# A sparse attention stage rearranged: indexer first, selection in parts, row-tile scores

## The chip, the cores and the metric

One program on one core of a Trainium2 chip. The metric is device time in microseconds for one launch, the median of three runs. The core's engines work side by side, each in the order of its own instruction stream: TensorE (PE, matmuls), VectorE (DVE), ScalarE (ACT), GpSimd (POOL), and SyncE (SP), which issues DMA transfers.

## The reference

The program is a chain of seven stages on 512 tokens of 1024 channels, all in float32: a feed-forward block, a hybrid mixer (dilated attention and mLSTM), a second feed-forward block, then a sparse attention mixer, a feed-forward block, a short convolution mixer and a last feed-forward block. The change touches the sparse attention alone:

```
q, k, v, qi, ki, wi = split(h @ w_in)       # 16 q heads, 4 k and v heads of 64;
                                            # 8 indexer heads qi of 64, one ki of 64, 8 weights wi
q = rope(rmsnorm(q));  k = rope(rmsnorm(k))
qi = rope(qi);  ki = rope(layernorm(ki))
for each block j of 128 queries:            # j = 0..3
    score = sum_h wi[:, h] * relu(qi[:, h] @ ki.T)       # (128, 512)
    score = where(causal, score, -inf)
    sel   = top_k(score, 128)               # the 128 best keys of each query
    p     = softmax over the selected, causal keys of q @ k.T / 8   # 4 q heads share a k head
    o     = p @ v
y = o @ w_out
```

Block j needs only its 128(j+1) causal keys, and block 0 needs no selection, since its causal keys are at most 128.

## The kernel before, in words

Activations lie with channels on the partitions and the 512 tokens along the row. A float32 projection is done as three matmuls of split operands (L461 to L463): a weight tile is cast to a high part on ACT (L124) and the rest is subtracted on DVE or POOL (L126). `W.pool_lo` says which: False all on DVE, True every second one on POOL, 2 all on POOL. Raw weights come in 1 MB loads on SP's queue (L101) into a ring of three buffers, so a load waits until the splits of an older one are done.

`proj_T` makes n output chunks of 128 channels; behind each chunk's 24 matmuls it evacuates the PSUM tile and calls `step()`. `step()` runs the callbacks that were put on `deferred` before, and advances the generator at the head of `side_work` by one. So each projection chunk carries a portion of other work, written out in the order in which the engines get it. There is no scheduler; the order in the program is the order on each engine.

The stage, `dsa_block` (L1453 to L1797), goes like this.

- ki and the four qi chunks are projected. `rope` swaps the 32-row halves by DMAs on SP (L1464, L1465), multiplies by cosine and sine on POOL (L1466, L1469), and adds on DVE (L1472). A head has 64 channels, so two heads lie on the 128 partitions of a chunk. For the two heads of a chunk to be scored by 128-partition matmuls, ki is copied on ACT into two tiles padded with zeros (L1526, L1527); the zeros are set on POOL (L1484, L1485). The keys k get the same treatment, eight copies into KZ (L1650, L1651).
- Beside the k and q projections the generator `select` (L1578) issues, in one step, two pairs of indexer products (L1557) and their readers: relu on ACT (L1565), the weighted sum on DVE (L1567, L1569). The top-k selection follows: 16 rounds for each of j = 1, 2, 3. A round is the eight largest of each row (MAX8, L1589) and their replacement by a mark (MATCH_REPLACE8, L1591), over 128(j+1) columns. PLAN sets how many rounds of j = 1 and 2 stand in a step, alternating instruction by instruction where both have some. The rounds of j = 3 come one to a step.
- The order of the projections is k, q (eight chunks), v. q's squares are summed by a matmul into one PSUM tile (L1628), and behind the last q chunk the roots of all are taken at once (L1704 to L1712).
- Attention follows in 32 units (j, hp), hp a pair of heads: first (1, hp) and (2, hp) alternating, then (3, hp) and (0, hp). A unit has scores (L1730), mask, scale and row minimum in one DVE instruction (L1738), exp with its sum on ACT (L364), division on POOL (L1748), transposes (L1757), copies (L1760), the products with v (L1770), and the split of the output (L1774, L1775). The loop is a pipeline: in one turn unit u gets its scores, u−1 its division, u−3 its transposes, u−5 its values. A unit that needs a selection not yet done makes the loop `step()` until it is. The output projection follows (L544).

Of the kernel before, what the change touches and what calls it, by code (L numbers as in the profile page):

```python
# [237 lines left out]
def body(ctx: ExitStack, tc: tile.TileContext, A: dict, consts: bass.AP, out: bass.AP,  # L238
# [11 lines left out]
    cl = ctx.enter_context(tc.tile_pool(name="col", bufs=8))  # L250
# [63 lines left out]
    mhalf = cp.tile([P, 4], F32, tag="mhalf", name="mhalf")  # L314
# [1138 lines left out]
    def dsa_block(layer):  # L1453
# [27 lines left out]
        kiA, kiB = big("U4"), big("U5")  # L1481
        KZ = [(big(f"U{6 + 2 * g}"), big(f"U{7 + 2 * g}")) for g in range(4)]
        def zeros(a, b):
            nc.gpsimd.memset(a[64:128], 0.0)  # L1484
            nc.gpsimd.memset(b[0:64], 0.0)  # L1485

        def evac_qi(c, ps):
            raw = tmp()
            nc.scalar.copy(raw, ps)
            rope(QI[c], raw)  # L1490
            zeros(*KZ[c])

# [3 lines left out]
        def evac_ki(c, ps):  # L1496
            raw = big("F4")
            nc.scalar.copy(raw[0:72], ps[0:72])
            zeros(kiA, kiB)
            x = raw[0:64]  # L1500

            def rest():
# [11 lines left out]
                def more():  # L1514
# [15 lines left out]
                    rope(x, z, 64, last)  # L1530
# [13 lines left out]
        marks = {}  # L1544

        def score(*heads):


            parts = []
            for j, h in heads:  # L1550
                n = P * (j + 1)
                if h == 0:
                    marks[j] = big(f"F{j}")
                both = pb("A") if not parts else None
                for i in range(2):
                    ps = both[:, S * i:S * i + n] if both is not None else pm()[:, 0:n]
                    nc.tensor.matmul(ps, QI[h // 2][:, P * j:P * (j + 1)], (kiA, kiB)[i][:, 0:n],  # L1557
                                     start=True, stop=True)
                    parts.append((j, h + i, ps))
            for j, h, ps in parts:  # L1560
# [18 lines left out]
        def select():  # L1579

            def some_scores():
                if ready and to_score:
                    score(*[to_score.pop(0) for _ in range(min(2, len(to_score)))])

            def rounds(j, n):
                sc = marks[j][:, 0:P * (j + 1)]
                for _ in range(n):
                    m8 = colt((P, 8))
                    nc.vector.max(m8, sc)  # L1589
                    yield  # L1590
                    nc.vector.match_replace(sc, m8, sc, TAKEN)  # L1591
                    yield

            def some_rounds(*many):
                todo = [rounds(*x) for x in many if x[1]]
                while todo:
                    todo = [x for x in todo if next(x, True) is None]

            def taken(j):
                sel[j] = sel_t[:, j - 1] if j < 3 else sel_u[:, 0]  # L1600
                n = P * (j + 1)
                nc.vector.tensor_scalar(sel[j][:, 0:n], marks[j][:, 0:n], -2e38, NEG, op0=ALU.is_gt, op1=ALU.mult)

            while len(to_score) > 8:
                some_scores()
                yield
            for n1, n2 in PLAN:
                some_rounds((1, n1), (2, n2))
                yield
                some_scores()  # L1610
            taken(1)
            taken(2)
            for _ in range(16):
                some_rounds((3, 1))
                yield
            taken(3)
# [5 lines left out]

        def squares(t, ps, start, stop):
            sq = side("acc", (P, S))
            nc.scalar.activation(sq, ps, AF.Square)

            def add():
                nc.tensor.matmul(ss[0:20, 0:S] if t >= 2 else ss[0:20, S:2 * S], zsel[:, t, :], sq,  # L1628
                                 start=start, stop=stop)

            deferred.append(add)

        kraw = [big("F5"), big("F0")]

        def evac_k(c, ps):
            nc.scalar.activation(kraw[c], ps, AF.Copy, scale=cB[:, 73:74])
            squares(c, ps, c == 0, c == 1)
            if c == 0:
                return

            def rest():
                v, y = tmp()[0:4], sp1.tile([P, 768], F32, tag="wide", name=nm("wide"))[0:4, 0:S]
                nc.vector.tensor_scalar(v, ss[0:4, S:2 * S], 1.0 / 64, EPS, op0=ALU.mult, op1=ALU.add)
# [4 lines left out]
                def copies(g):  # L1648
                    (a, b), o = KZ[g], kraw[g // 2][64 * (g % 2):64 * (g % 2) + 64]
                    nc.scalar.copy(a[0:64], o)  # L1650
                    nc.scalar.copy(b[64:128], o)  # L1651
                    if g < 3:
                        deferred.append(lambda: copies(g + 1))

                def more():
                    for t in range(2):
                        p1 = pm()

                        nc.tensor.matmul(p1, kexp[t], y, start=True, stop=True)
                        o, z = kraw[t], side("ada_w", (P, 768))[:, 0:S]  # L1660
                        nc.vector.tensor_tensor(z, o, p1, op=ALU.mult)
                        rope(o, z, then=(lambda: copies(0)) if t else None)

                deferred.append(more)

            deferred.append(lambda: deferred.append(lambda: deferred.append(rest)))

        side_work.append(select())
        W.pool_lo = True
        proj_T("dsa", 2, H, evac_k)  # L1670
        Q = [big(f"U{14 + i}") for i in range(8)]

        def evac_q(c, ps):
            raw = side("ada_w", (P, 768))[:, 0:S]
            nc.scalar.activation(raw, ps, AF.Copy, scale=cB[:, 72:73])
            squares(2 + c, ps, c == 0, c == 7)
            rope(Q[c], raw)

        V = [big("F6"), big("F7")]

        def evac_v(c, ps):
# [3 lines left out]
            def rest():  # L1685
# [3 lines left out]
                for jj in range(2):  # L1689
                    nc.scalar.copy(V[jj].rearrange("p (j c) -> p j c", j=2)[:, :, P * c:P * (c + 1)],  # L1690
                                   pt[:, 256 * jj:256 * (jj + 1)].rearrange("p (j c) -> p j c", j=2))
# [3 lines left out]
        rows, rq = big("F4"), big("R", F32, (P, 80))  # L1695

        def sums_out():
            step()
            nc.scalar.copy(rows[0:20], ss[0:20, 0:S])

        def roots():


            ps = pm()  # L1704
            for j in range(NT):
                nc.tensor.transpose(ps[:, 20 * j:20 * (j + 1)], rows[0:20, P * j:P * (j + 1)], ident[0:20, 0:20])
            v, t = tmp(), tmp()
# [5 lines left out]

        proj_T("dsa", 8, H, evac_q)
        midway.extend([sums_out, roots])
        W.pool_lo = 2
        proj_T("dsa", 2, H, evac_v)


# [213 lines left out]
```

## Time and profile before

| what | value |
|---|---|
| median of 3 runs | 2681.61 us (2677.54 to 2684.05) |
| profiled execution, its own time | 2684.03 us |
| its span, first to last instruction | 2682.3 us, 32412 instructions |
| mean granted TensorE clock | 0.993 of full |
| PE busy over the span | 2635.3 us (98%), 12880 matmuls |
| DVE busy | 1385.7 us (52%) |
| ACT busy | 918.2 us (34%) |
| POOL busy | 541.9 us (20%) |
| DMA | 288.43 MB, mean 108 GB/s |

The sparse attention stage lies between about 1486 and 1740 us of the span; in the page's row of 40 slices its place is the 23rd to 26th slice. Busy shares over the whole span say little about it: the other stages are long runs of projections. Matmul ends in the trace are modelled and overlap, so intervals between starts are used for PE. Lines such as L1730 are lines of the kernel before.

### The profile page before, as it was taken

The numbers are of one execution on the slowest core, as the hardware profiler recorded it, in microseconds if no ns is written. First come the engines' busy times: TensorE is split into PE (matmuls) and PEld (weight loads), VectorE is DVE, ScalarE is ACT, GpSimd is POOL, SyncE is SP. The second block draws the span as 40 slices with busy tenths as digits, with TensorE's granted clock in tenths as the row PEclk, the third lists the DMA queues.
The fourth block names the chain that finished last, engine by engine and source line by source line (L and its number), as shares of the span: only waits on it lengthen the run. The fifth ranks groups of instructions, "written<-read, shape, count | busy, mean of one in ns | idle before, by whom it ended". The sixth has DMA issues, their size and how long they took to land.

```text
span 2682.3 us, 32412 instructions
## 1 busy us (share of the span) xinstructions
PE 2635.3 (98%) x12880; PEld 2174.9 (81%) x12880; DVE 1385.7 (52%) x2072; ACT 918.2 (34%) x1482; POOL 541.9 (20%) x548
## 2 busy tenths in 40 slices
PE   8999999999999999999999899999999999999999
PEld 7888889888777788888888766788888888888887
DVE  5545566375627454665555689453333544533332
ACT  4322233322344433423223436532222332322222
POOL 3211234154112211422123445220000200200000
PEclk9999999999999999999999899999999999999999
DMA  6555443223221323246545131032232322232322
GB/s 187 158 180 185 143 146 118 63 71 95 73 69 48 110 83 122 86 154 199 187 152 160 43 101 60 8 104 87 87 110 75 115 94 96 86 98 83 111 85 71
DMA packets 256474, 288.43 MB, mean 108 GB/s; under 512 B 9924, under 2 KB 238836, under 8 KB 256324
## 3 DMA queue, kind: packets, MB, share of 16 engines
q1 hardware_dynamic: 244196, 234.91, 28.0%
q0 software_dynamic: 10496, 50.95, 6.1%
q8 instruction: 101, 1.65, 0.3%
q10 hardware_dynamic: 1632, 0.52, 0.1%
q14 instruction: 49, 0.40, 0.0%
HBM read 278.59 MB, written 4.19 MB: 105 GB/s over the span
## 4 chain that ended last, share of the span: by engine, by line
PE 90%; DVE 7%; ACT 1%; issue 1%; POOL 1%; DMA 0%; SPq 0%; DVEq 0%; ACTq 0%; POOLq 0%
PE mm L461 25%; PE mm L462 25%; PE mm L463 25%; PE mm L544 2%; PE mm L657 1%; PE mm L659 1%; PE mm L658 1%; PE mm L1730 1%; PE B L1136 1%; DVE X L810 1%; DVE L L696 1%; PE mm L1770 1%; PE A L1279 1%; PE B L1302 1%; DVE F L1591 1%
## 5 line engine op out<-in xcount | busy, mean ns | idle before, releaser
L461 PE MATMUL mm<-H,whi 128*128 128x512 f32 (+1 forms) x2360 | 902.3, 382 | 0.0
L462 PE MATMUL mm<-L,whi 128*128 128x512 f32 (+1 forms) x2360 | 893.7, 379 | 1.4 <-DVE L L696 1.4
L463 PE MATMUL mm<-H,wlo 128*128 128x512 f32 (+1 forms) x2360 | 893.4, 379 | 0.9 <-DVE wlo L126 0.9
L126 DVE TENSOR_TENSOR wlo<-raw,whi 128x1024 fp32r<-128x1024 f32 (+3 forms) x431 | 505.9, 1174 | 555.0 <-ACT whi L124 550.8
L124 ACT CAST whi<-raw 128x1024 fp32r<-128x1024 f32 (+3 forms) x460 | 444.6, 968 | 411.4 <-PE mm L462 332.0
L461 PEld LDWEIGHTS mm<-H,whi 128*128 128x128 f32 x2360 | 445.5, 189 | 91.5 <-issue 10.6
L463 PEld LDWEIGHTS mm<-H,wlo 128*128 128x128 f32 x2360 | 445.3, 189 | 84.2 <-DVE wlo L126 1.6
L462 PEld LDWEIGHTS mm<-L,whi 128*128 128x128 f32 x2360 | 445.8, 189 | 83.6 <-DVE L L696 2.2
L461 PE MATMUL mm<-U,whi 128*128 128x512 f32 (+1 forms) x804 | 312.4, 389 | 0.0
L463 PE MATMUL mm<-U,wlo 128*128 128x512 f32 (+1 forms) x804 | 310.8, 387 | 0.0
L462 PE MATMUL mm<-U,whi 128*128 128x512 f32 (+1 forms) x804 | 310.7, 386 | 0.0
L413 POOL TENSOR_TENSOR acc<-acc,sq 128x512 f32<-128x512 f32 (+1 forms) x74 | 91.9, 1241 | 642.4 <-ACT sq L400 641.7
L670 ACT CAST U<-t 128x512 fp32r<-128x512 f32 x104 | 64.6, 621 | 406.9 <-POOL t L759 194.2
L461 PEld LDWEIGHTS mm<-U,whi 128*128 128x128 f32 x804 | 151.0, 188 | 33.5 <-issue 3.3
L463 PEld LDWEIGHTS mm<-U,wlo 128*128 128x128 f32 x804 | 151.0, 188 | 30.8
L462 PEld LDWEIGHTS mm<-U,whi 128*128 128x128 f32 x804 | 151.0, 188 | 30.2
L671 DVE TENSOR_TENSOR U<-t,U 128x512 fp32r<-128x512 f32 x104 | 72.1, 693 | 134.2 <-ACT U L670 134.2
L882 POOL DMA_DIRECT2D ada_w<-in_ada_w_dram x128 | 71.5, 558 | 281.6 <-DVE wide L906 220.5
L906 DVE SCALAR_TENSOR_TENSOR wide<-ada_w,csilu,wide 128x768 f32<-128x768 f32 x112 | 115.3, 1029 | 16.2 <-DMA ada_w<-in_ada_w_dram 16.2
L126 POOL TENSOR_TENSOR wlo<-raw,whi 128x1024 fp32r<-128x1024 f32 (+1 forms) x29 | 69.5, 2398 | 247.2 <-ACT whi L124 245.6
L757 DVE TENSOR_TENSOR t<-t,mm 128x512 f32<-128x512 f32 x88 | 60.3, 685 | 110.9 <-PE mm L463 110.8
L759 POOL TENSOR_TENSOR t<-t,R 128x512 f32<-128x512 f32 x44 | 56.4, 1283 | 218.4 <-DVE t L757 211.2
(386 smaller groups left out, 2791.7 us busy)
## 6 DMA issues: line engine op xcount, KB each, us to landing
ada_w<-in_ada_w_dram POOLq DMA_DIRECT2D x128, 384.0 KB, 3.6
raw<-in_ffn_w_up_dram SPq DMA_DIRECT2D x44, 1024.0 KB
raw<-in_ffn_w_gate_dram SPq DMA_DIRECT2D x43, 1024.0 KB
raw<-in_w_in_dram SPq DMA_DIRECT2D x30, 1024.0 KB
raw<-in_ffn_w_down_dram SPq DMA_DIRECT2D x32, 768.0 KB
raw<-in_ffn_w_down_dram SPq DMA_DIRECT2D x32, 640.0 KB
raw<-in_w_in_dram SPq DMA_DIRECT2D x24, 512.0 KB
raw<-in_conv_w_in_dram SPq DMA_DIRECT2D x12, 1024.0 KB
```

The costliest lines, as they stand in the source:

```text
L124: nc.scalar.copy(hi, raw)
L126: e.tensor_tensor(lo, raw, hi.bitcast(F32), op=ALU.subtract)
L413: (eng or nc.vector).tensor_tensor(self.acc[:, c], self.acc[:, c], sq[:, c], op=ALU.add)
L461: nc.tensor.matmul(ps, whi, hhi, start=start, stop=False)
L462: nc.tensor.matmul(ps, whi, hlo, start=False, stop=False)
L463: nc.tensor.matmul(ps, wlo, hhi, start=False, stop=stop)
L670: nc.scalar.copy(hi, src)
L671: nc.vector.tensor_tensor(lo, src, hi.bitcast(F32), op=ALU.subtract)
L757: nc.vector.tensor_tensor(s, s, ps, op=ALU.mult)
L759: nc.gpsimd.tensor_tensor(s, s, R, op=ALU.mult)
L882: nc.gpsimd.dma_start(loaded[i], A["ada_w_2"][layer, k * P:(k + 1) * P, 768 * cg:768 * (cg + 1)])
L906: nc.vector.scalar_tensor_tensor(acc, w, csilu[:, k:k + 1], acc, op0=ALU.mult, op1=ALU.add)
```

## The change

Only `dsa_block` changes, the order of its weights, and the number of small buffers. In its order:

- **ki and products.** ki stands once on partitions 0 to 63 and is brought to 64 to 127 by a DMA on SP's queue, in the step in which ki's rotation ends. Products are 64-row tiles: the two heads of a chunk on the two halves of the partitions, each into its own PSUM half, 256 columns at a time. A step issues products (`some_products`), and the next step their readers (`weighed`). The flag `ready` is set one step earlier than before.
- **Selection.** One generator goes through j = 1, 2, 3 in order; each round yields a cost estimate, and `select(much)` runs rounds until a budget is spent: 5.0 a step, 2.4 + 1.6 where units are under way beside q, 1.4 a turn of the loop behind q. j's rounds begin when all its products have been weighed.
- **Keys.** The rotated keys are used as they are; `KS` holds them with the two halves exchanged, by four DMAs on SP.
- **Order.** k, then v, then q. q's squares are matmuls with the squares stationary, into eight columns of PSUM tile B for each chunk; the roots are taken per chunk, by one DVE instruction and five small POOL ones.
- **Units.** Blocks 0 and 1 are one unit, so there are 24: eight (0,1), eight (2), eight (3). Up to six of the first kind start beside the q projections (`beside_q`); their outputs go to `kept` and are split later (`parted`). Scores, too, are row tiles.
- **lo splits.** `W.pool_lo = 2` is gone, so every second split stays on DVE up to the end of the attention.

```diff
@@ plan_dsa
     plan.append(chunk_T("dsa", w, 0, ND, C["k"], 256))
+    plan.append(chunk_T("dsa", w, 0, ND, C["v"], 256))
     plan += [chunk_T("dsa", w, 0, ND, C["q"] + 256 * c, 256) for c in range(4)]
-    plan.append(chunk_T("dsa", w, 0, ND, C["v"], 256))
@@ dsa_block
...
                     def last():
-                        nc.scalar.copy(kiA[0:64], x)
-                        nc.scalar.copy(kiB[64:128], x)
-                        deferred.append(lambda: deferred.append(lambda: ready.append(True)))
+                        nc.sync.dma_start(ki[HALF[1]], ki[HALF[0]])
+                        deferred.append(lambda: ready.append(True))
...
+        def products(heads, ps):
+            j, h = heads
+            n = P * (j + 1)
...
+            for o in range(0, n, 256):
                 for i in range(2):
-                    ps = both[:, S * i:S * i + n] if both is not None else pm()[:, 0:n]
-                    nc.tensor.matmul(ps, QI[h // 2][:, P * j:P * (j + 1)], (kiA, kiB)[i][:, 0:n],
+                    c = slice(o, min(o + 256, n))
+                    nc.tensor.matmul(ps[i][:, c], QI[h // 2][HALF[i], P * j:P * (j + 1)], ki[HALF[i], c],
                                      start=True, stop=True)
...
-        PLAN = ((6, 0), (6, 0), (4, 4), (0, 4), (0, 4), (0, 4))
+        def selection():
+            for j in (1, 2, 3):
+                n = P * (j + 1)
+                while j not in whole:
+                    yield 100.0
+                sc = marks[j][:, 0:n]
+                for r in range(16):
                     m8 = colt((P, 8))
                     nc.vector.max(m8, sc)
                     nc.vector.match_replace(sc, m8, sc, TAKEN)
+                    yield 0.3 + n / 470
...
+            def swapped(t):
+                for i in range(2):
+                    nc.sync.dma_start(KS[t][HALF[i]], kraw[t][HALF[1 - i]])
...
+            def add():
+                both = bank()[:, 384:392]
+                for j in range(NT):
+                    nc.tensor.matmul(both[:, 2 * j:2 * j + 2], sq[:, P * j:P * (j + 1)], zsel[:, 2, 4:6], start=True,
+                                     stop=True)
+                def rest():
+                    v, y, z = colt((P, 8)), colt((P, 8)), colt((P, 8))
+                    nc.vector.tensor_scalar(v, both, 1.0 / 64, EPS, op0=ALU.mult, op1=ALU.add)
+                    nc.gpsimd.tensor_tensor(y, v, mhalf, op=ALU.pow)
...
+                    there[0] = c + 1
...
-        units = [(j, hp) for hp in range(8) for j in (1, 2)] + [(j, hp) for hp in range(8) for j in (3, 0)]
+        units = [((0, 1), hp) for hp in range(8)] + [((2,), hp) for hp in range(8)] + [((3,), hp) for hp in range(8)]
...
         def scores(u):
...
-                nc.tensor.matmul(ps[:, 0:n], Q[hp][:, P * j:n], KZ[hp // 2][i][:, 0:n], start=True, stop=True)
+            for j, o in places(js):
+                n = P * (j + 1)
+                for c in range(0, n, 256):
+                    w = min(256, n - c)
+                    for i in range(2):
+                        nc.tensor.matmul(pss[i][:, o + c:o + c + w], Q[hp][HALF[i], P * j:P * (j + 1)],
+                                         k2[i][HALF[i], c:c + w], start=True, stop=True)
...
+        def beside_q():
+            while True:
+                go(6)
+                go(4)
+                go(1)
+                if parts:
+                    weighed()
+                now = at[0] - at[2]
+                select(2.4 if now else 5.0)
+                go(2)
+                if now:
+                    select(1.6)
+                while adds:
+                    adds.pop(0)()
+                go(5)
+                go(3, at[2] - 1)
+                banks.clear()
+                if sel[1] is not None and at[0] < 6 and there[0] > at[0] + 1:
+                    go(0)
+                some_products()
+                yield
...
+        side_work.append(beside_q())
+        W.pool_lo = True
+        proj_T("dsa", 2, H, evac_k)
+        proj_T("dsa", 2, H, evac_v)
+        proj_T("dsa", 8, H, evac_q)
+        side_work.clear()
...
+        while at[6] < len(units):
+            go(5, now - 4)
+            go(6)
+            go(3, now - 2)
+            go(0)
+            go(2, now)
+            now += 1
+            go(4)
+            if at[1] < len(units):
+                while sel[units[at[1]][0][-1]] is None:
+                    if parts:
+                        weighed()
+                    some_products()
+                    select(2.0)
+            go(1)
+            if waiting:
+                hp = waiting.pop(0)
+                parted(hp, slice(0, 256), kept[hp // 2][:, hp % 2])
+            select(1.4)
             step()
```

`go(stage)` moves the next unit through one of the seven stages scores, softmax, divided, transposed, copied, values, put.

## Rows read from the trace of the kernel before

**Rows 1.** the chain of waits over the whole span: shares by engine.

```profile
PE 90%; DVE 7%; ACT 1%; issue 1%; POOL 1%; DMA 0%; SPq 0%; DVEq 0%; ACTq 0%; POOLq 0%
```

**Rows 2.** stretches: start:end, length; busy us of PE, PEld, DVE, ACT, POOL; PEclk.

```profile
1535.00:1558.00 23.00, 18.44 (x69) 12.71 (x68) 11.88 (x16) 11.63 (x21) 9.18 (x9) 0.93 0.42 123
1558.00:1665.00 107.00, 101.54 (x453) 65.08 (x453) 100.62 (x256) 56.11 (x134) 53.15 (x49) 0.97 0.28 82
1665.00:1718.00 53.00, 52.92 (x418) 35.27 (x419) 28.17 (x125) 42.42 (x149) 22.31 (x42) 1.00 0.01 1
```

**Rows 3.** DVE by line and form, 1558 to 1665: busy us, mean ns.

```profile
L1589 DVE MAX8 col<-F 128x8 f32<-128x512 f32 x16 | 11.0, 688 | 0.0
L1591 DVE MATCH_REPLACE8 F<-col,F 128x512 f32<-128x512 f32 x16 | 10.8, 676 | 0.0
...
L126 DVE TENSOR_TENSOR wlo<-raw,whi 128x1024 fp32r<-128x1024 f32 x4 | 7.3, 1818 | 1.3 <-ACT whi L124 1.3
L1738 DVE CUSTOM_DVE_ANT_0 t<-mm,U,R 128x384 f32<-128x384 f32 x12 | 6.9, 606 | 0.1
...
L1738 DVE CUSTOM_DVE_ANT_0 acc<-mm,U,R 128x256 f32<-128x256 f32 x7 | 3.3, 467 | 0.0
```

**Rows 4.** DVE in time (start us, us): first rounds, last round.

```profile
1558.01 0.41 DVE L1589 MAX8 col<-F 128x8 f32<-128x256 f32 x1
...
1558.98 0.43 DVE L1589 MAX8 col<-F 128x8 f32<-128x256 f32 x1
...
1663.96 0.68 DVE L1591 MATCH_REPLACE8 F<-col,F 128x512 f32<-128x512 f32 x1
```

**Rows 5.** PE in time: steady units, then the output projection's first matmul.

```profile
1669.94 1.46 PE L1730 MATMUL mm<-U,U 128*128 128x384 f32 x4
1671.32 0.32 PE L1770 MATMUL mm<-wide,F 128*64 128x128 f32 x1
...
1672.84 1.88 PE L1730 MATMUL mm<-U,U 128*128 128x512 f32 x4
...
1677.79 1.88 PE L1730 MATMUL mm<-U,U 128*128 128x512 f32 x4
...
1717.23 0.92 PE L544 MATMUL mm<-H,whi 128*128 128x256 f32 x3
```

**Rows 6.** PE in time, two 4-row tiles side by side, in the mix stage.

```profile
756.74 0.69 PE L1257 MATMUL A<-rc,cst 4*128 4x512 f32 x1
756.74 0.69 PE L1258 MATMUL A<-rc,cst 4*128 4x512 f32 x1
757.27 0.59 PE L1257 MATMUL A<-rc,cst 4*128 4x512 f32 x1
```

**Rows 7.** all engines in time around ki (SPq: SP issuing a DMA).

```profile
1531.57 3.79 DVE L126 TENSOR_TENSOR wlo<-raw,whi 128x1024 fp32r<-128x1024 f32 x1 [1.66 <-ACT whi L124]
...
1535.28 0.68 DVE L1472 TENSOR_TENSOR F<-F,t 64x512 f32<-64x512 f32 x1
...
1538.47 0.58 SPq L101 DMA_DIRECT2D raw<-in_attn_w_in_dram  x1
...
1539.23 0.51 SPq L1464 DMA_DIRECT2D t<-t  x1
...
1545.52 1.29 POOL L1469 TENSOR_TENSOR t<-t,rs 128x512 f32<-128x512 f32 x1 [1.86 <-DMA t<-t]
```

**Rows 8.** waits of SP's queue, 1535 to 1720: us in total, times, longest.

```profile
SPq L101 <- POOL wlo L126: 13.1, 1, 13.1
```

**Rows 9.** PE in time at 1535, and the stretch behind it (PEclk eighth).

```profile
1534.77 0.39 PE L462 MATMUL mm<-L,whi 128*128 128x512 f32 x1
1534.99 0.39 PE L463 MATMUL mm<-H,wlo 128*128 128x512 f32 x1
1539.92 1.89 PE L1628 MATMUL B<-acc,dsa_consts 128*20 128x512 f32 x2 [4.54 <-ACT acc L1625]
...
1540.00:1550.00 10.00, 9.98 (x34) 6.59 (x35) 5.34 (x8) 3.35 (x8) 4.83 (x5) 0.83 0.75 233
```

More of the change, by code (lines that the diff above doesn't have):

```diff
@@ L1574, in score, with some_products @@
                                             compare_op=ALU.is_ge, fill=NEG)
-        PLAN = ((6, 0), (6, 0), (4, 4), (0, 4), (0, 4), (0, 4))
+                    whole.append(j)
+            parts.clear()
+        whole = []
         to_score = [(j, h) for j in (1, 2, 3) for h in (0, 2, 4, 6)]
[L1579 to L1587, printed above, removed]
+        def some_products():
+            if not ready or not to_score:
+                return
+            if to_score[0][0] == 1:
+                both = pb("A")
+                for k in range(2):
+                    products(to_score.pop(0), [both[:, S * i + 256 * k:S * i + 256 * (k + 1)] for i in range(2)])
+            else:
+                both = pb("A")
+                products(to_score.pop(0), [both[:, S * i:S * (i + 1)] for i in range(2)])
@@ L1611, in select @@
[L1611 to L1616, printed above, removed]
+                yield 0.5
+        selecting = selection()
+        def select(much):
+            while much > 0:
+                cost = next(selecting, None)
+                if cost is None:
+                    break
+                much -= cost
         ss = pb("B")
@@ L1646, in rest @@
                 newton(y, v, 1.0, tmp()[0:4])
[L1648 to L1670, printed above, removed]
+                deferred.append(lambda: more(y))
+            def add():
+                nc.tensor.matmul(ss[0:20, 0:S], zsel[:, c, :], sq, start=c == 0, stop=c == 1)
+                if c:
+                    deferred.append(rest)
+            deferred.append(add)
         Q = [big(f"U{14 + i}") for i in range(8)]
+        there = [0]
+        rq = big("R", F32, (P, NT, 16))
         def evac_q(c, ps):
@@ new lines, in divided, with width, transposed @@
+        def divided(u):
+            prs, l, some = probs[u]
+            nc.vector.reciprocal(l[:, 0:len(some)], l[:, 0:len(some)])
+            for k, pr in enumerate(some):
+                nc.gpsimd.tensor_scalar(pr, pr, l[:, k:k + 1], 0.0, op0=ALU.mult, op1=ALU.add)
+        def width(u):
+            return sum(P * (j + 1) for j in units[u][0])
+        def transposed(u):
+            ps = bank() if phase[0] else pb("AB"[u % 2])
+            for i, pr in enumerate(probs.pop(u)[0]):
+                for b in range(0, width(u), P):
+                    nc.tensor.transpose(ps[:, S * i + b:S * i + b + P], pr[:, b:b + P], ident)
+            turns[u] = ps
@@ L1777, in dsa_block @@
-        for u in range(len(units) + 5):
-            if 0 <= u - 5:
-                values(u - 5)
-            if 0 <= u - 3 < len(units):
-                transposed(u - 3)
-            if 0 <= u - 1 < len(units):
-                divided(u - 1)
-            if u < len(units):
-                while sel[units[u][0]] is None:
-                    step()
-                scores(u)
+            for x, (j, o) in enumerate(places(js)):
+                for b in range(j + 1):
+                    for i in range(2):
+                        nc.tensor.matmul(ob[64 * i:64 * i + 64, P * x:P * (x + 1)],
+                                         V[b // 2][:, 256 * (b % 2) + 64 * kv:256 * (b % 2) + 64 * kv + 64],
+                                         pts[i][:, o + P * b:o + P * (b + 1)], start=(b == 0), stop=(b == j))
@@ new lines, in dsa_block, with go @@
+        kept, waiting = {}, []
+        phase = [True]
+        stages_of_units = (scores, softmax, divided, transposed, copied, values, put)
+        at = [0] * len(stages_of_units)
+        def go(stage, most=len(units)):
+            if at[stage] < min(most, at[stage - 1] if stage else len(units)):
+                stages_of_units[stage](at[stage])
+                at[stage] += 1
+        def beside_q():
[19 more added lines that the diff above has]
+                yield
```

209 lines of the change are left out of this document (102 added, 107 removed).

## The prediction

> **What bounds the kernel now.** I read the chain of waits first: TensorE (PE) carries nine tenths of the chain that ended last, VectorE (DVE) most of the rest [rows 1]. The change lies in one stage, sparse attention, so I then cut that stage into stretches. The reader is to see two regimes [rows 2]. From 1558 to 1665 DVE is busy 100.6 of 107 us: the top-k rounds run from 1558.0 to 1664.6 [rows 4]. PE is busy 101.5 us there, but much of that is matmuls that found their operands just in time, and its clock is below full (0.97). From 1665 on DVE is busy 28 of 53 us and PE 52.9 of 53, up to the output projection at 1717.2 [rows 5]. So the stage is DVE-bound, then PE-bound: saved matmul time counts at full only behind the last round, and anything on DVE counts before it. A third place is a hole of 4.5 us on PE at 1535, after which 1540 to 1550 runs at a mean granted clock of 0.83, between its two levels (1.2 and 2.4 GHz) [rows 9].
>
> **The change, part by part.**
>
> *PE work behind the last round.* In the steady part a (j=2) unit costs 1672.84 − 1669.94 = 2.90 us of PE: 1.38 scores (to 1671.32), 1.52 values and transposes [rows 5]. Less 0.10 that I take for the change of shape, its four 384-column passes (two heads, two passes each in float32) make 1.28, 0.32 a pass; four of 512 columns by that 4 × 0.43 = 1.72. A (3)+(0) pair takes 4.95 us (1672.84 to 1677.79). After, a head's scores contract over 64 partitions instead of 128, two heads side by side on the two halves. What two side-by-side tiles cost stands in the trace once: two 4-row tiles of 512 columns start together, and the next pair starts 757.27 − 756.74 = 0.53 us later [rows 6], where two full passes take 0.86. That is 61%; some of the 0.53 I put down to the change of shape around it and take 56%. So a (2) unit costs 0.72 + 0.10 for the change of shape + 1.52 = 2.34, and a (3) unit, scaled by 4/3, 0.96 + 0.10 + 2.03 = 3.09. The Trainium skill (TensorEngine Tiling (Array Packing), section Overview, Theoretical Speedup) promises up to a factor 2 for a contraction of at most 64; the one pair in this trace shows 1.6. With the factor 2 the sum below ends 1.3 us earlier.
>
> *DVE work up to the last round.* Rounds keep their number, 16 for each of three blocks, 0.97 us at 256 columns [rows 4], 0.69 + 0.68 plus a load of the eight values, about 1.45, at 512 [rows 3]. Before interleaves part of j=1 and j=2, which I read as hiding some issue gaps; the sequential form loses them: +2.3 us, and nothing at the least. The lo splits: POOL takes all of them from the v projection on in before; now they alternate to the end, so DVE gets one more before its last round: 7.3/4 = 1.8 us [rows 3], at most two, 3.6. Softmax: before does 12 (2) and 13 (1) heads' reductions in this stretch (0.61 and 0.47 us each [rows 3]). After must, by my reading of the budgets (two rounds at 1.4 in the tail), have done about eight (0,1) units and one or two (2) units when the last round ends. A (0,1) unit takes 2 × 0.47 + 2 × 0.33 (0.47 less the 0.14 that 128 columns make between the two rows) + four readouts and a reciprocal, about 0.5, = 2.1 us, plus the split of its output: together +3 us. Rope adds, relu accumulation, k's Newton steps and the per-q roots (eight small DVE instructions against five) cost what they did. Sum +7 us on 107. Before's idle share (6.4 us) I take as a third smaller, since steps are larger and readers come a step later: −2.
>
> *When the rounds start.* After, the first products are issued a step earlier, right behind k0's projection, but need ki in its second partition half, brought by a DMA on SP's queue. ki's add ends at 1536.0 (DVE came to it only after a lo split that took 3.79 us beside two POOL instructions) [rows 7]. In order behind it on SP stand qi2's transfers, a 1 MB weight load issued at 1538.5, and qi3's transfers at 1539.2, whose reader on POOL starts at 1545.5 [rows 7]. The swap is issued between that load and qi3's transfers; they ran behind the load's packets, so I put it at about 1542.8. PE, ready at about 1529.7, would wait 13 us instead of 4.5, with k1's projection behind it. It costs little, since DVE starts its rounds at about 1557 in either: products (1,4) and (1,6) come right behind k1's projection, near 1552, as in before, and before's first round waited for a lo split. Bounds: the swap lands at once, rounds 5 us earlier; it lands behind a second load, 5 us later. What is late next is k1, by 8 us, covered by PE's slack in the DVE-bound stretch.
>
> *PE in that stretch.* Indexer products halve (about −7 us), q's squares become eight small matmuls per chunk, about the same; k, v and q still make eleven projections behind k0's first. A projection is 24 matmuls that start 0.22 to 0.23 us apart [rows 9], 5.45 us. Before, PE had from 1535 on ten of them (54.5), 16 unit pairs of (1) and (2) and of (3) and (0) at some 4.9 (79), and 29 for products, squares and small things: 162. After, from 1529.7 on: eleven (60), 16 units of 2.34 and 8 of 3.09 (62), products 9.4, the rest 12.5: 144. Nothing of it shows while DVE is the bound.
>
> *POOL and ACT.* Ten POOL memsets and ten ACT copies vanish, five small POOL instructions per q come. POOL is busy 53 of 107 us [rows 2], so they are hidden, unless they hold DVE up: DVE's lo split took 3.79 us beside POOL against 1.8 on average [rows 3, 7]. The Trainium skill (SBUF — State Buffer, section on the two separate sides) says that DVE and GpSimd share a port pair as an exclusive lock and that the loser blocks for the whole instruction; the trace agrees in that row. By that rule 40 more POOL instructions would stretch DVE's two-input ones; with a quarter of DVE's time in such, an estimate of 4 us later. The sum leaves it out.
>
> *Sum.* Last round: 1557 + 107 + 7 − 2 = 1669. Then 14 units lack scores, 17 transposes, 19 values: 6 × 2.34 + 8 × 3.09 = 38.8, plus 3 × 0.75 + 5 × 0.8 = 6.3 for the older units (half of a (2) unit's 1.52 each), plus 1 for the drain: 46.1. End 1715.1 against 1717.2: −2.1. The profiled execution took 2684.0 (span 2682.3 and 1.7 around it), 2.4 above the median of 2681.6; so 2681.9 by it, and **2680 on the median**.
>
> Both ends: with perfect overlap PE never waits but for ki's swap, and the stage ends at 1529.7 + 144 + 13 = 1687, −30. If 12 us of DVE work more than I see come in front, +10.
>
> **The rivals.**
>
> *R1, faster: selection goes under the projections and PE, not DVE, sets the end.* For it: DVE's 114 us fit beside eleven projections and the units if rounds are spread well; up to six (0,1) units run beside q and bring PE work into what was slack. Against it: j=3's selection can't start until all its products are in, about q7. By 1529.7 + 144 + 13 + some 10 of remaining waits the stage ends at 1697: −20, **2661**.
>
> *R2, slower: the swaps on SP's queue starve DVE.* Besides ki's, four transfers turn k's halves, also on SP, also between weight loads; in before SP once stood 13.1 us at a load that waited for a lo split on POOL [rows 8]. If a swap is issued behind such a load, the first scores stop PE, the projections and products behind them wait, and DVE runs out of work after one step's budget, about 6 us. It decides from a wait of some 9 us at the scores; a 13.1 us wait costs about 7 net, two of them or one plus a later ki about 12: **2692**. Against it: k's swaps are issued four or more projections before their readers.
>
> *R3, row tiles do not run side by side.* Then the 14 units' scores cost 6 × 0.56 + 8 × 0.76 = 9.4 us more: **2689**. For it: the tiles of the trace have 4 rows and stream 512 columns, these have 64 and 256. Against it: two tiles on different partitions did start together [rows 6].
>
> *R4, the change doesn't do what it says:* no unit starts beside q, because sel[1] or the roots come too late. Then DVE has the same work in another order: 2683.
>
> **How the numbers follow.** No change 0.44 (own range 2670 to 2690), R1 0.31, R2 0.12, R3 0.09, R4 0.04. Less than 0.3% (8 us) is not to be told from nothing. Faster: R1 and 0.08 of the first, 0.39. Slower: R2, 0.06 of R3, 0.04 of the first, 0.22. Same: 0.39. The range reaches from a good R1 to R2, 2656 to 2698.
>
> **What would show it.** In the profile after: the first round near 1557 and the last near 1669 (R1: before 1655; R2: after 1675); PE's wait at the first products about 13 us, released by a DMA; a (3) unit at 3.1 us of PE (R3: 3.9); about 14 units' scores behind the last round; other stages unchanged. The forecast is wrong if the rounds' stretch is far from 112 us or if PE waits behind it.

## The result, and the profile after

The changed kernel takes 2709.7 us in the median (2706.7 to 2711.0), against 2682.2 for the kernel before: a ratio of 1.0104, 95% interval 1.0086 to 1.0121. It is 27.5 us slower. The forecast was no change, at 2680, with a range up to 2698.

The two traces first need a common mark. ACT's copy of ki out of PSUM stands at the same place of both programs, in the kernel before and in the kernel after at:

```profile
1512.13 0.58 ACT L1498 COPY F<-mm 72x512 f32<-72x512 f32 x1 [2.52 <-PE mm L463]
```

```profile
1506.34 0.58 ACT L1498 COPY F<-mm 72x512 f32<-72x512 f32 x1 [2.50 <-PE mm L463]
```

So a time of the trace after is read 5.8 us later to compare it with a time of the trace before or of the forecast. The change does not make this shift: over the nineteen traces of this document the copy lies anywhere between 1505.3 and 1512.5, in versions of either kernel.

The stretches of the profile after that answer to [rows 2]; columns as there, PEclk the eighth: first round to last round, then up to the output projection.

```profile
1554.40:1693.10 138.70, 107.77 (x561) 82.49 (x559) 107.28 (x271) 52.73 (x139) 73.68 (x99) 0.82 0.23 67
1693.10:1740.00 46.90, 46.06 (x473) 36.02 (x473) 26.51 (x97) 39.19 (x112) 20.06 (x32) 1.00 0.01 2
```

DVE's work between the rounds is 107.3 us, against 100.2 to 100.6 before: the +7 of the forecast, though not from the terms that it was added up from (see below). The part behind the last round is 46.9 us, forecast 46.1. What is wrong is the length of the first line: 138.7, not 112. DVE stands idle for 31 us of it (before: 6), PE too, and PE's mean granted clock there is 0.82 (before: 0.97).

From ki's copy to the output projection, the kernel before and the kernel after:

```profile
1512.13:1717.20 205.07, 194.99 (x1048) 130.78 (x1046) 153.78 (x405) 118.86 (x314) 96.99 (x112) 0.98 0.22 66
```

```profile
1506.34:1740.00 233.66, 188.67 (x1189) 144.18 (x1187) 158.50 (x394) 109.34 (x279) 111.24 (x143) 0.86 0.21 60
```

PE's busy time fell by 6 us only, and much of it now runs at a lower granted clock (0.86 in the mean, 0.98 before); its idle time grew from 10 to 45 us. The sum is 28.6 us, near the 27.5 of the medians. The two spans (2682.3 and 2704.9) differ by 22.6, which is 28.6 less the shift of 5.8 ahead of the stage.

Where PE waits in the profile after, 1554.4 to 1693.1 (total, times, longest):

```profile
PE B L1681 <- DVE col L1686: 13.0, 2, 10.8
PE B L1785 <- DVE col L1774: 6.8, 1, 6.8
PE B L1681 <- ACT U L1796: 6.0, 2, 4.3
PE mm L1748 <- DVE L L671: 2.9, 1, 2.9
```

and where DVE waits in the same stretch:

```profile
DVE col L1605 <- POOL F L1575: 9.1, 3, 5.4
DVE F L1571 <- ACT sq L1567: 6.0, 4, 1.8
DVE L L671 <- ACT H L670: 4.2, 2, 3.0
```

The longest wait shows how the two stop each other. DVE in time (start, duration, and in brackets the idle time before it):

```profile
1579.34 0.29 DVE L1609 TENSOR_SCALAR U<-F 128x256 bf16<-128x256 f32 x1
...
1588.05 4.05 DVE L1571 SCALAR_TENSOR_TENSOR F<-sq,wcol,F 128x384 f32<-128x384 f32 x2 [1.41 <-ACT sq L1567]
1597.50 0.56 DVE L1605 MAX8 col<-F 128x8 f32<-128x384 f32 x1 [5.40 <-POOL F L1575]
```

```profile
1603.64 1.22 DVE L126 TENSOR_TENSOR wlo<-raw,whi 128x1024 fp32r<-128x1024 f32 x1
1604.77 1.29 DVE L1472 TENSOR_TENSOR F<-F,t 128x512 f32<-128x512 f32 x2
...
1605.97 0.69 DVE L1472 TENSOR_TENSOR U<-U,t 128x512 f32<-128x512 f32 x1
1606.57 0.16 DVE L1686 TENSOR_SCALAR col<-B 128x8 f32<-128x8 f32 x1
...
1606.88 0.77 PE L1681 MATMUL B<-dsa_consts,acc 128*128 128x2 f32 x3 [10.75 <-DVE col L1686]
```

j=1's rounds are done at 1579.3 (L1609 is its `taken`). j=2's can't start before its four pairs of products, issued one pair a step, have been weighed and POOL has set the causal mask (L1575): 1597.5, 18 us later. (Before j=3's rounds there is a second such hole, of 10.9 us.) Then five rounds, a lo split and three rope adds stand ahead of L1686, the read that frees PSUM tile B for PE's next squares. PE has been done with its projection since 1596 and waits till 1606.9. The clock follows:

```profile
1590.00:1600.00 10.00, 6.13 (x30) 4.49 (x26) 4.36 (x8) 4.02 (x6) 8.38 (x11) 1.00 0.43 133
1600.00:1610.00 10.00, 3.12 (x16) 3.05 (x18) 9.62 (x22) 0.00 (x0) 2.86 (x6) 0.54 0.26 62
1610.00:1620.00 10.00, 10.00 (x48) 7.80 (x47) 8.29 (x22) 3.92 (x13) 8.76 (x9) 0.78 0.07 17
1660.00:1670.00 10.00, 4.94 (x24) 3.48 (x24) 5.77 (x25) 4.76 (x19) 9.67 (x13) 0.50 0.37 117
```

Idle PE, a granted clock near its lower level, and work after that at 0.78. The same at 1660 to 1670, where the last q chunks come through POOL (9.67 of 10 us busy).

At the start PE waits 5.3 us for ki's rope add on DVE (L1472) and, as forecast, another 7.9 for ki's exchange (L1525), which stands on SP's queue behind a weight load:

```profile
1529.47 1.22 PE L1555 MATMUL A<-U,U 64*128 64x256 f32 x2 [5.32 <-DVE U L1472]
...
1531.93 0.58 SPq L101 DMA_DIRECT2D raw<-in_attn_w_in_dram  x1
1532.62 0.56 SPq L1525 DMA_DIRECT2D U<-U  x1
...
1538.60 2.07 PE L1555 MATMUL A<-U,U 64*128 64x256 f32 x6 [7.90 <-DMA U<-U]
```

The units themselves came out well. PE in the steady part, answering to [rows 5]: first a (2) unit, then a (3) unit, each from its first score matmul to that of the next.

```profile
1705.05 0.48 PE L1748 MATMUL mm<-U,U 64*128 64x256 f32 x1
1705.06 0.48 PE L1748 MATMUL mm<-F,U 64*128 64x256 f32 x1
1705.37 0.38 PE L1748 MATMUL mm<-U,U 64*128 64x256 f32 x1
1705.38 0.38 PE L1748 MATMUL mm<-F,U 64*128 64x256 f32 x1
...
1705.59 0.27 PE L1748 MATMUL mm<-U,U 64*128 64x128 f32 x1
...
1707.52 0.48 PE L1748 MATMUL mm<-U,U 64*128 64x256 f32 x1
...
1727.34 0.48 PE L1748 MATMUL mm<-U,U 64*128 64x256 f32 x1
...
1730.46 0.48 PE L1748 MATMUL mm<-U,U 64*128 64x256 f32 x1
...
1739.97 0.62 PE L544 MATMUL mm<-H,whi 128*128 128x256 f32 x3
```

A (2) unit takes 2.47 us (forecast 2.34, before 2.90), a (3) unit 3.12 (forecast 3.09). Two heads' passes of 256 columns, started 0.01 us apart, together take 0.22 us (1705.37 to 1705.59), where one head's 384 took 0.32 before, or 0.21 for 256. That is the full factor of 2 that the Trainium skill (TensorEngine Tiling (Array Packing), Overview, Theoretical Speedup) names as the upper end; here the trace agrees with it.

### The profile page after: what moved, and what is told of

The parts are those of the page before. It is cut to its first block, busy times and chain, and to the rows that moved or that the text cites. A ratio compares the mean times of both kernels' runs of the same rounds, so it can differ in the third digit from the quotient of the medians.

```text
span 2704.9 us, 32602 instructions
## 1 busy us (share of the span) xinstructions
PE 2625.6 (97%) x13020; PEld 2186.4 (81%) x13020; DVE 1389.4 (51%) x2060; ACT 908.7 (34%) x1447; POOL 554.0 (20%) x577
## 4 chain that ended last, share of the span: by engine, by line
PE 88%; DVE 7%; POOL 1%; ACT 1%; issue 1%; DMA 1%; SPq 0%; DVEq 0%; ACTq 0%; POOLq 0%
PE mm L461 25%; PE mm L462 25%; PE mm L463 25%; PE mm L544 2%; PE mm L657 1%; PE mm L658 1%; PE mm L659 1%; DVE col L1605 1%; DVE F L1606 1%; PE B L1136 1%; DVE X L810 1%; DVE L L696 1%; PE mm L1748 1%; PE mm L1807 1%; PE A L1279 1%
```

## The experiments

Medians, and ratios to the kernel before that ran on the same chip, with 95% intervals:

| run | us | ratio |
|---|---|---|
| after | 2709.7 | 1.0104 (1.0086 to 1.0121) |
| 2 rounds, after | 2684.2 | 1.0009 (0.9999 to 1.0018) |
| 2 rounds, before | 2673.6 | 0.9968 (0.9959 to 0.9978) |
| 2 rounds, after, exchanges on ACT's queue | 2673.8 | 0.9974 (0.9963 to 0.9985) |
| half budget | 2693.0 | 1.0045 (1.0030 to 1.0060) |
| quarter budget | 2693.7 | 1.0043 (1.0027 to 1.0060) |
| two pairs of j=2 in a step | 2696.4 | 1.0051 (1.0036 to 1.0066) |
| read before rounds | 2700.9 | 1.0072 (1.0057 to 1.0087) |
| exchanges on ACT's queue | 2706.6 | 1.0090 (1.0075 to 1.0105) |
| half budget + exchanges | 2686.8 | 1.0021 (1.0011 to 1.0031) |
| half budget + exchanges + two pairs | 2687.9 | 1.0020 (1.0011 to 1.0030) |
| no units beside q | 2707.8 | 1.0094 (1.0075 to 1.0112) |
| no units beside q, v last | 2708.4 | 1.0104 (1.0088 to 1.0119) |
| the same, read first, budget 4.0 | 2698.7 | 1.0070 (1.0053 to 1.0087) |
| roots off POOL | 2713.6 | 1.0124 (1.0109 to 1.0139) |
| four edits | 2696.7 | 1.0063 (1.0048 to 1.0078) |
| row tiles in the old order | 2680.0 | 0.9990 (0.9980 to 0.9999) |
| row tiles and merged units in the old order | 2672.5 | 0.9958 (0.9943 to 0.9973) |

**Is it the rounds?** In both kernels 2 rounds a block instead of 16, so that 16 keys a query are selected, not 128. In the kernel after it is the line below, in the kernel before PLAN and the loop over j=3's rounds.

```diff
-                for r in range(16):
+                for r in range(2):
```

> The changed kernel with 2 selection rounds instead of 16 for each block (it selects 16 keys, not 128): some 52 us of DVE work left out. If DVE's rounds, by their length or by standing ahead of reads, hold the stage up, what is left is set by PE (144 us of work from 1530 on, 13 us wait at ki): 2660 to 2675, no less gain than the same edit brings in the kernel before. If the time is lost in waits that have nothing to do with the rounds (swap, steps, POOL): 2680 to 2695.

> The kernel before with 2 selection rounds instead of 16 for each block (16 keys, not 128), the counterpart of the run above. PE has 162 us of work from 1535 to the output projection and 182 us of time, so at most 20 us can be won here: 2664 to 2676. Both theories expect the same of it; it gives the length of the stage where PE alone sets it, so that the PE work saved by the change can be read from the pair.

The rounds cost the kernel after 25.5 us and the kernel before 8.9. So some 17 of the 27.5 us come from how the rounds lie among the rest. 10.5 us are there without them, though PE has less to do. Neither case of the expectation covers both parts: the time, 2684.2, is that of the second (waits that have nothing to do with the rounds), the gain, larger than in the kernel before, that of the first.

**How much of them stands together.** Half and a quarter of the budget beside q.

```diff
-                select(2.4 if now else 5.0)
+                select(1.2 if now else 2.5)
...
-                    select(1.6)
+                    select(0.8)
```

> The changed kernel with half the round budget in each step beside q (2.5 for 5.0; 1.2 + 0.8 for 2.4 + 1.6), the budget behind q unchanged. Theory L: shorter blocks of rounds before each read, PE's waits at tile B fall to less than half of 26 us, q ends some 10 us earlier; the rounds that are left come behind q, two to a unit: 2695 to 2706. Rival D (DVE's time is lost where it has no round to do): DVE idles more beside q, more rounds are left, 2712 to 2722.

> The changed kernel with a quarter of the round budget beside q (1.2 for 5.0; 0.6 + 0.4 for 2.4 + 1.6): one or two rounds in a step. Lockstep theory: half the budget took most of it, so beside q PE waits no less than with half, while more rounds are left for the tail: 2690 to 2702. If the loss grew simply with rounds beside q: another 8 us less, 2682 to 2688.

Half gives 16.7 us back, a quarter no more. With half, PE's wait for L1686 falls from 13.0 to 0.5 us, and the part behind the last round from 46.9 to 32.2, since more units are done by then. But the half budget does two things: shorter blocks, and j=1's rounds last until j=2 is ready. j=2's first round comes 91.6 us behind ki's copy (91.2 with the full budget), but the hole of 18.2 us ahead of it is down to 0.2. The next two runs part the two.

```diff
+                two = to_score[0] == (2, 0)
                 both = pb("A")
...
+                if two:
+                    products(to_score.pop(0), [pm(), pm()])
```

> The changed kernel with two pairs of j=2's products in one step (the second pair in two ordinary PSUM tiles), so that j=2's rounds can begin a step earlier; budgets as changed. Rival D (DVE starves between j=1's last round at 1579.6 and j=2's first at 1597.5): the hole halves, 2698 to 2704. Lockstep theory: the same rounds come as large blocks ahead of the reads, only earlier: 2705 to 2712.

13.3 us back with blocks as long as ever. DVE's wait for j=2 shrinks; in this kernel (L1612 is `taken`, L1608 the round, L1689 the read of the squares):

```profile
1585.61 0.30 DVE L1612 TENSOR_SCALAR U<-F 128x256 bf16<-128x256 f32 x1
...
1592.39 0.56 DVE L1608 MAX8 col<-F 128x8 f32<-128x384 f32 x1 [1.43 <-POOL F L1575]
```

```profile
PE B L1684 <- DVE col L1689: 5.0, 2, 4.7
```

6.8 us instead of 18.2, and PE's wait for the read is 5.0 instead of 13.0. My rival was right here: DVE without rounds to do is the larger cause (13.3 us, against 8.8 in the next run; the two overlap), and the long block ahead of the read is what turns it into a wait of PE.

```diff
                 now = at[0] - at[2]
+                while adds:
+                    adds.pop(0)()
                 select(2.4 if now else 5.0)
...
-                while adds:
-                    adds.pop(0)()
...
-                deferred.append(rest)
+                rest()
```

> The changed kernel with one edit: in each step beside q the squares' matmuls and DVE's read of them come before the rounds of the step, no longer behind the rounds of the step before; units start as early as in the changed kernel. Theory L (lockstep: PE stands at PSUM tile B for that read, 19 us in all, its clock falls, and DVE then waits for PE): PE's waits at the squares nearly vanish, the last round comes 10 us earlier or more, 2692 to 2702. Rival D (DVE is kept from its rounds by the order of the selection, since a block's rounds wait for all its products): PE runs ahead and waits at another place, 2706 to 2713.

8.8 us back, with the hole before j=2 as long as ever (17.6 us), and PE's waits moved rather than vanished:

```profile
PE B L1785 <- DVE col L1686: 10.1, 3, 6.6
PE mm L1748 <- DVE F L1472: 8.9, 1, 8.9
```

The second is the keys' rope add, which stood behind the same rounds. So block length counts too, but at each read that PE waits for, not at one.

**The exchange of ki.**

```diff
-                        nc.sync.dma_start(ki[HALF[1]], ki[HALF[0]])
+                        nc.scalar.dma_start(ki[HALF[1]], ki[HALF[0]])
...
-                    nc.sync.dma_start(KS[t][HALF[i]], kraw[t][HALF[1 - i]])
+                    nc.scalar.dma_start(KS[t][HALF[i]], kraw[t][HALF[1 - i]])
```

> The changed kernel with the transfers that exchange halves (ki's one, the keys' four) issued on ACT's queue instead of SP's, so that they don't stand behind weight loads and rope transfers. Rival S (the late swap costs what PE waits for it, 13 us): 2696 to 2702. Theory L: PE's wait at the first products shrinks by 4 to 8 us, but what follows is set by DVE and tile B, so 2704 to 2711.

> The changed kernel with 2 rounds instead of 16 for each block (16 keys selected, not 128) and the exchanges on ACT's queue; to be read against the run with 2 rounds alone (2684.2) and the kernel before with 2 rounds (2673.6). Theory: of the 10.5 us that the changed kernel loses without rounds, PE's wait at ki's exchange (13 us against 4.5) is the larger part, and with no rounds to take up the time won it shows: 2675 to 2679. Rival (what remains is the small units' chain behind q, or POOL): 2681 to 2686.

> The changed kernel with half the round budget beside q and the exchanges on ACT's queue. With the full budget the exchange alone gave 3 us, with almost no rounds 10. If the rounds' blocks had swallowed the rest, half the budget lets more of it through: 2683 to 2688. If the two share one wait: 2690 to 2694.

PE's wait for ki's transfer falls from 7.9 us (7.7 with 2 rounds) to 1.5 in each. The edit moves the keys' four transfers too, but in the profile after PE has no wait for those. With all rounds that brings 3 us, with half the budget 6, with 2 rounds 10.3: there the medians of the two kernels are equal, 2673.8 and 2673.6. 10.3 us is more than the wait that went, and from ki's copy to the output projection the traces show less. With 2 rounds, after, before, and after with the exchanges on ACT's queue:

```profile
1511.50:1717.31 205.81, 179.66 (x1188) 138.79 (x1186) 107.90 (x268) 109.28 (x279) 114.80 (x143) 0.90 0.23 69
```

```profile
1510.98:1709.19 198.21, 192.18 (x1048) 129.87 (x1046) 110.25 (x279) 119.17 (x314) 96.99 (x112) 0.98 0.23 68
```

```profile
1508.64:1709.21 200.57, 180.37 (x1188) 138.87 (x1186) 108.09 (x268) 109.31 (x279) 115.51 (x143) 0.91 0.24 70
```

In the stage the exchange brings 5.2 of 7.6 us. So the late exchange is the larger part of what is lost without rounds, and with all rounds a part of it is hidden.

> The run before this and two pairs of j=2's products in one step. With half the budget j=1's rounds last until j=2 is weighed, so the hole that the two pairs close is closed already: no more than 3 us better than the run before. If the early start of j=2 counts by itself: another 8 to 13 us, 2672 to 2679.

No further gain: the hole before j=2 was closed already by the half budget (0.2 us without the two pairs and with them). The three edits together leave the kernel 0.2% above the one before.

**What did not count.** Units beside q, the order of v (the weights are put into the same order), and POOL:

```diff
-                if sel[1] is not None and at[0] < 6 and there[0] > at[0] + 1:
+                if sel[1] is not None and at[0] < 0 and there[0] > at[0] + 1:
...
-        proj_T("dsa", 2, H, evac_v)
         proj_T("dsa", 8, H, evac_q)
+        proj_T("dsa", 2, H, evac_v)
```

> The changed kernel without units beside q: all 24 start behind the q projections, everything else as changed. Theory L (the units' transposes, tile B, their copies on ACT and the squares share queues and a PSUM tile with the q projections, so PE and DVE stop each other there): PE's waits between the q projections fall below 10 us, q's last projection ends before 1640, the last round comes near 1675, 2685 to 2698. Rival D (units beside q fill PE where DVE is the bound; without them their PE work comes behind the last round): 2712 to 2725.

> The changed kernel without units beside q and with the order k, q, v of the kernel before, nothing else; to be read against the run without units (2707.8). Theory J (join): behind the last q projection PE has nothing to do while that q's rotation (transfers, POOL, DVE) and roots come through, and its clock falls; v's two projections, 11 us, cover that in the kernel before. Then 2692 to 2700. If the join costs nothing, the order makes no difference: 2704 to 2712.

> Row tiles, merged units, sequential selection of the changed kernel, but no units beside q, order k, q, v, squares and their read before the step's rounds, round budget 4.0 instead of 5.0 a step. If lockstep at tile B and the join make up the loss, both are gone and the PE work saved is left: 2670 to 2686. If the loss lies in the selection order or elsewhere: 2690 to 2705.

The first line of the edit alone changes the time by 2 us (PE's wait for L1686 grows to 25.4), all of it by 1. My theory of the join falls: v behind q does not help. The third run reads the squares first as well. Its last round ends at 1673.8, counted from ki's copy 24 us earlier than in the changed kernel, but no unit has run, and all 24 lie behind it:

```profile
1673.80:1731.70 57.90, 57.90 (x582) 45.18 (x581) 32.88 (x132) 50.17 (x152) 26.88 (x48) 0.99 0.01 2
```

57.9 us at a full PE instead of 46.9. The run is 11 us faster than the changed kernel: of an early last round that is bought with units, 11 us are lost again behind it.

```diff
-                    nc.gpsimd.tensor_tensor(y, v, mhalf, op=ALU.pow)
+                    act(y, v, AF.Ln)
+                    act(y, y, AF.Exp, scale=-0.5)
```

(the four instructions behind it likewise on DVE)

> The changed kernel with the roots of each q chunk taken by ACT (Ln, Exp) and DVE (four small instructions) instead of POOL's five, of which the power alone takes 1.6 to 1.8 us. Theory P (POOL's queue, busy 4.7 of 5 us at the join and late with the causal mask that DVE's rounds wait for, 9 us, is a part of the loss): 2694 to 2703. Without it, DVE's and ACT's added instructions cost 0 to 5 us: 2708 to 2716.

> The changed kernel, units beside q kept, with four edits together: read before rounds, half the round budget beside q, roots off POOL, exchanges on ACT's queue. If their causes are separate, the gains add up (9 + 17 + some 8 + 3, less what two of them share): 2678 to 2690. If they are one wait seen at several places, no better than the budget alone: 2690 to 2696.

Roots off POOL: 4 us slower, with overlapping intervals, so at least no gain. DVE's wait for POOL's causal mask does fall, from 9.1 to 1.2 us, but the hole before j=2 is still 16.2 us, DVE is busy for 118 us between first and last round instead of 107, and it waits 5.0 us for ACT's part of the roots. All four together are worse by 10 us than budget and exchanges alone: reads first, roots on DVE, or both take back what the others give.

**The useful parts alone,** in the kernel before: first row-tile scores and exchanged keys, then also blocks 0 and 1 in one unit.

```diff
-                nc.tensor.matmul(ps[:, 0:n], Q[hp][:, P * j:n], KZ[hp // 2][i][:, 0:n], start=True, stop=True)
+            for c in range(0, n, 256):
+                w = min(256, n - c)
+                for i in range(2):
+                    nc.tensor.matmul(pss[i][:, c:c + w], Q[hp][HALF[i], P * j:n], k2[i][HALF[i], c:c + w],
+                                     start=True, stop=True)
...
-        units = [(j, hp) for hp in range(8) for j in (1, 2)] + [(j, hp) for hp in range(8) for j in (3, 0)]
+        units = [x for hp in range(8) for x in (((0, 1), hp), ((2,), hp))] + [((3,), hp) for hp in range(8)]
```

> The kernel before with the units' scores alone done as row tiles, keys exchanged by four transfers on SP instead of eight zero-padded copies; nothing else of the change. If two row tiles run side by side at full rate, the PE-bound part behind the last round loses half the score time of eight (3), eight (0) and some (2) units, about 10 us: 2668 to 2675. If they don't, or if the transfers on SP hold the keys up: 2680 to 2690.

> The kernel before with two parts of the change, row-tile scores and blocks 0 and 1 in one unit ((0,1) and (2) alternating, then eight (3)); order, selection, squares and lo splits as before. Row tiles alone gave 0.1%, with 4.7 us for a (3)+(0) pair where PE needs about 4.1. With (3) units alone behind the last round at 2.9 to 3.0 us, and eight (0) parts brought in front of it (about 8 us of DVE): 2670 to 2678. If the DVE part grows by more than the tail shrinks: 2680 to 2686.

Row tiles alone give 0.1%: a (3)+(0) pair still takes 4.7 us. With merged units the kernel takes 2672.5 us, 0.42% below the kernel before and 37 below the changed one. Its stretches:

```profile
1552.10:1662.40 110.30, 105.33 (x533) 70.09 (x532) 104.67 (x278) 56.75 (x150) 56.63 (x61) 0.95 0.29 85
1662.40:1701.90 39.50, 39.45 (x400) 30.23 (x398) 21.93 (x86) 33.88 (x100) 17.57 (x30) 1.00 0.01 2
```

DVE is idle for 5.6 of 110 us; 13 us are gone behind the last round [rows 2].

## Why the prediction was wrong

The failing step is one term of the sum: "Before's idle share (6.4 us) I take as a third smaller, since steps are larger and readers come a step later: −2." It rose to 31.4: +25, where I had −2. What the runs showed in its place: DVE has no round to run for 18.2 us before j=2 and 10.9 before j=3, since a block's rounds wait for its last product, and PE then stands behind DVE's queue. In the list of DVE's waits that is 9.1 us for POOL's mask and 6.0 for ACT's relus, and later 4.8 for scores of PE, which was late by then. With this term fails "Nothing of it shows while DVE is the bound": DVE was busy 107 of 139 us, so it was not the bound, and each wait of PE counted.

- *PE's work behind the last round* (46.1) was right, 46.9, and so was its working: the scores of fourteen units lie there.
- *DVE's work* (+7) came out by luck. The rounds, put at +2.3, are busy for 57 us in both kernels. The weighted sums, said to cost what they did, take 7.5 us more, and the rope adds give 3.1 back (10.3 to 7.2). Before, then after:

```profile
L1569 DVE SCALAR_TENSOR_TENSOR F<-sq,wcol,F 128x384 f32<-128x384 f32 x7 | 6.2, 883 | 0.6
L1569 DVE SCALAR_TENSOR_TENSOR F<-sq,wcol,F 128x512 f32<-128x512 f32 x7 | 5.3, 751 | 1.4 <-ACT sq L1565 0.7
```

```profile
L1571 DVE SCALAR_TENSOR_TENSOR F<-sq,wcol,F 128x384 f32<-128x384 f32 x7 | 10.4, 1493 | 1.8 <-ACT sq L1567 1.4
L1571 DVE SCALAR_TENSOR_TENSOR F<-sq,wcol,F 128x512 f32<-128x512 f32 x7 | 8.6, 1225 | 5.0 <-ACT sq L1567 4.6
```

- *The first round* came at 1554.4, or 1560.2 counted from ki's copy as in the trace before (forecast 1557), the last at 1693.1, or 1698.9 (1669). My own test, "the forecast is wrong if the rounds' stretch is far from 112 us", was met.
- *The exchange of ki*: a wait of 13 us at PE was forecast and 13.2 came, 5.3 of it for ki's add and 7.9 for the transfer. "It costs little, since DVE starts its rounds at about 1557 in either" holds with all rounds, 3 us; with half the budget the same edit brings 6, so other waits had taken the gain up.
- R1's counter-argument, "j=3's selection can't start until all its products are in", named the right mechanism, but I applied it to j=3 only, and only against a gain. j=3 has its hole of 10.9 us, and at j=2 the same rule made the one of 18 us. Its working was at hand: one pair a step, four pairs, steps of 7 to 9 us, against 16 rounds of 0.97 us.
- R2 had the right sign and the wrong place: it was not the keys' transfers on SP that starved DVE but the order of products, and what stopped PE was DVE's in-order queue.
- R3 is not borne out: the tiles run side by side at the full factor, and a (3) unit takes 3.12 us.
- Of the port rule the trace shows the effect, but not where I looked. DVE's weighted sums are long where POOL works on a whole tile: two of them take 1.33 us by themselves; with POOL's lo split and rope beside them a single one takes 2.49.

```profile
1574.16 1.33 DVE L1571 SCALAR_TENSOR_TENSOR F<-sq,wcol,F 128x384 f32<-128x384 f32 x2
```

```profile
1587.76 2.36 POOL L126 TENSOR_TENSOR wlo<-raw,whi 128x1024 fp32r<-128x1024 f32 x1
1588.05 2.49 DVE L1571 SCALAR_TENSOR_TENSOR F<-sq,wcol,F 128x384 f32<-128x384 f32 x1 [1.41 <-ACT sq L1567]
1590.08 1.60 POOL L1469 TENSOR_TENSOR t<-t,rs 128x512 f32<-128x512 f32 x1
```

The small root instructions themselves do not lengthen it: beside L1687 a weighted sum of 512 columns takes 0.75 us, as by itself. With the roots off POOL the fourteen sums take 13.6 us instead of 19.0, yet that kernel is not faster, so what the long sums cost the time is not shown.

What stays open: with half the budget and the exchanges 5 us are missing to the kernel before and 14 to the merged version, with the two pairs added 6 and 15. A wait of PE of 4.6 to 6.9 us at the first transposes behind q, for DVE's reciprocal (L1774), is in the kernel after and in the variants of budget, pairs and exchanges; no run took it away alone.

## What to carry to other kernels

When a phase bound by one engine is rearranged, its idle time is the term to work out, step by step: when is the first instruction of each block of work ready, and what stands in the queue ahead of the result that another engine waits for. A budget per step does no good where the next block is not yet allowed to start. Cut a rearrangement into its parts: here the part that saved work was worth 0.4% in the old order, and the rest of the change cost 1.4%.

## What the runs showed of the hardware

- In the profile after, POOL's power of 128x8 elements takes 1.81 us (L1687 at 1606.81), against 0.20 for each of the three products behind it on the same tile size.
- Around PE's wait of 10.75 us (1596.1 to 1606.9) the mean granted clock is 0.54 in the stretch 1600 to 1610 and 0.78 in the next 10 us: near the lower of the two levels (1.2 and 2.4 GHz), then between them. The projection at 1611.9 takes 6.8 us, the one at 1582.9, ahead of the wait, 5.6.
- A 128 KB transfer within the chip, issued 0.7 us behind a 1 MB weight load on the same queue, was there for its reader 6.0 us after its issue (1532.62 to 1538.60); on ACT's queue, which carries no weight loads there, PE's wait for it falls from 7.9 to 1.5 us.
- A two-input DVE instruction of 128x384 elements takes 0.6 us by itself and up to 2.6 us beside POOL's work on whole tiles (L1571 in the profile after).
